# A hybrid pooling and Mamba-2 layer: the last pool gate placed ahead of the output's last part, late products tile by tile, and two sets of weight sums moved into the pool stage

## The chip, the core and the metric

The kernel runs on one core of one Trainium2 chip. The metric is device microseconds of one launch; the figure for a kernel is the median of its runs. The engines are named as the profile names them: PE (matrix products), PEld (its weight loads, which overlap it), DVE (vector), ACT (scalar), POOL (GpSimd, here used nearly only to issue DMAs) and SP (sync, which issues most of the weight loads).

## The reference, cut to what matters

One layer (D = 1024, 512 tokens behind 16 learned ones) with two branches on the same normalised input, merged by gates and followed by an MLP with a squared ReLU:

```python
u = rmsnorm(h, mix_norm_w)
proj = u @ w_in                      # columns: u_pool, z, xBC, dt, gates
gates = sigmoid(proj[..., OFF_GATE:] + b_gate)      # 2 x 1024 columns
# pooling branch: 4 groups of 256 channels, causal mean over 2, 4, 8, 16 tokens
#   minus the input, times a 256 x 256 weight per group, times a scale
y_pool = pool_mixer(u_pool, pool_w_group, pool_scale) @ w_pool_up
# Mamba-2 branch: conv + silu, chunked state-space scan in 8 groups of 256
#   channels, times silu(z), RMS-normalised by group
y_ssd = mamba2_branch(z, xbc, dt_raw, ...) @ w_ssd_out      # 2048 -> 1024
h = h + (gate_pool * y_pool + gate_ssd * y_ssd) @ w_o
v = rmsnorm(h, mlp_norm_w)
hid = relu(v @ w_ff1)                # 1024 -> 4096
h = h + (hid * hid) @ w_ff2          # 4096 -> 1024
out = rmsnorm(h, final_norm_w)
```

## The kernel before, in words

Everything is float32. A product is made of three products of rounded parts: each operand is split into a rounded "hi" half (cast on ACT: yh, whi, ph, ...) and the remainder "lo" (subtraction on DVE: yl, wlo, pl, ...), and hi x hi, lo x hi and hi x lo are added up in PSUM. Some weights go through a seven-product scheme of the Strassen kind; it needs sums of weight blocks. Those of w_ff1 and w_ff2 are made ahead of time by DMAs alone: `weight_steps` (L770) issues, on POOL's queue, copies and accumulating DMAs of 512 KB from one place of device memory to another. A set of w_ff1 ("f1") takes eight of them, in four steps that depend on one another (t1, then t1 += , t2 += t1, t4 += t2), a set of w_ff2 ("f2") four. An accumulating DMA is issued only when the copy under it has landed, and POOL stands in its queue until then. Of the last four sets (f1 4, f2 5, f1 5, f2 6) SETS_POOL (L56) says how many are issued in the pool stage; it is 0 before, and all four follow the load of the residual ht (L1202).

In the order of time:

- **Scan, groups 0 to 7** (to about 474 us): projection, conv, scan and normalisation by group of 256 channels. Each group leaves two tiles of y (y0, y1 of group 0 to y14, y15 of group 7), split into yh and yl at the end of `ssd` (the loop behind `rs`, L719 to L726). A planner of the framework orders the instructions by the order in which they are written, by what they wait for, and by `tc.high_priority` where that is set; `weave` alternates the written order of a scan with that of a filler.
- **The filler of group 7** is `out_part` (L845): w_ssd_out by y8 to y13, in eight output tiles psp0 to psp7 of 128 channels x 512 tokens. They share two PSUM buffers, so psp2 may start when psp0 has been copied out. For each, `add` (L870) copies it on ACT to a tile sp and adds it to `acc_d` in device memory by an accumulating DMA on POOL's queue. psp0 and psp1 are begun before y12 and y13 (group 6) exist; their "late products" (L880 to L883) come when those are there.
- **Pool stage** (474 to 555 us): `pool_pair` makes the u_pool channels of one group of 256 (numbers 3, 2, 1, 0 in that order) by seven products: its weights come as two raw tiles per pair (`raw_block`, L126), are added up on DVE (`sm`, L985 and L987, and back into raw, L989 and L990) and split (whiA, whiS, whiD, whiB on ACT, wlo* on DVE). `averaged` (L962 to L964) makes the causal means on DVE, `pooled_halves` (L973, L974) splits them into ph and pl, `pool_mix` (L1043) multiplies by the group's weight (pg). Between pairs 3 and 2 stand the last part of the output, psl0 to psl7 (y14 and y15 by w_ssd_out, six matmuls each, four PSUM buffers), added to acc0 to acc7 on DVE (L1067), and the last pool gate, `gate_pool(7)`: 24 matmuls into pgp, and a sigmoid on ACT (L759) into m1[7]. The other seven gates have been in device memory since the scan and are loaded to m1 by POOL's queue (L1090).
- **Merge, w_o, MLP** (555 to 1000 us): w_pool_up with the gates, w_o, then ff1 blocks 0 to 3 as plain products, with the start of ff2's seven products woven in (its alpha, L1533, feeds the residual ht on DVE, L1240), then the seven-product MLP.

The weights of w_in-shaped blocks come in a list (`blocks`, filled by `_weight_blocks`) in the order of their use; `block()` takes the next: a raw tile of 128 x 1024 (three buffers, so a load on SP's queue waits until an earlier raw tile's lo half has been made), then whi on ACT (L111) and wlo on DVE (L113).

Of the kernel before, what the change touches and what calls it, by code (L numbers as in the profile page):

```python
# [9 lines left out]
F32 = mybir.dt.float32  # L10
# [4 lines left out]
P = 128  # L15
# [39 lines left out]
PIECES = {4: 21, 7: 14}  # L55
SETS_POOL = 0  # L56

# [7 lines left out]
def kernel(ctx: ExitStack, tc, xT, x, w, fx, f1, f2, vec, fnw, out):  # L65
# [100 lines left out]
    def col(off, i, n=P):  # L166
        return vs[:n, off + i : off + i + 1]
# [426 lines left out]
    def ssd(g, cur):  # L594
# [123 lines left out]
        yield  # L718
        for i in range(2):  # L719
            y = yt[:, i, :]  # L720
            dve.scalar_tensor_tensor(y, y, col(V_SN, 2 * g + i), rs, op0=ALU.mult, op1=ALU.mult)
            yh = yp.tile([P, SEQ], F32R, tag="yh", name=f"yh{g}_{i}")
            yl = yp.tile([P, SEQ], F32R, tag="yl", name=f"yl{g}_{i}")
            act.copy(yh, y)
            dve.tensor_tensor(yl, y, yh.bitcast(F32), op=ALU.subtract)
            ys.append((yh, yl))  # L726
        yield
# [114 lines left out]
    def out_part():  # L842
# [36 lines left out]
        late = [[(next(un), ys[k]) for k in (12, 13)] for d in range(2)]  # L879
        for o in ((0, 0), (1, 0), (0, 1)):  # L880
            for d in range(2):
                for n, (a, b) in enumerate(late[d]):
                    pe.matmul(ps[d], a[o[0]], b[o[1]], start=False, stop=o[1] == 1 and n == 1)  # L883
            yield
        for d in range(2):
            add(ps[d], d)
        for d in range(2, NK):
# [167 lines left out]
    for d in range(NK):  # L1055
        t_load = nc.gpsimd.dma_start(acc[d], acc_d[d])
    for _ in range(SETS_POOL):
        with tc.issue_after(t_load.ins):
            t_load = weight_sums()
    pend = [pooled_halves(*a) for a in pool_pair(POOL_ORDER[0])]  # L1060

    un = units()
    psl_add = []
# [5 lines left out]
    wgb = block(psl_add[2])  # L1069
    gate_pool(NK - 1)  # L1070
    pool_mix(POOL_ORDER[0], pend, wgb)
    nxt = pool_pair(POOL_ORDER[1], psl_add[:2])
    gts = []
    for n in range(1, 4):
# [11 lines left out]
        if n == 1:  # L1086
            for d in MERGE:
                with tc.issue_after(mixed[0].ins):
                    if d < NK - 1:
                        nc.gpsimd.dma_start(m1[d], gate_d[d])  # L1090
    pool_stack.close()
# [602 lines left out]
def _weight_blocks(i):  # L1694
# [9 lines left out]
    def put(b):  # L1704
        blocks.append(b)
# [39 lines left out]
    for t in range(2):  # L1745
        put(cols(w_in, (2 * POOL_ORDER[0] + t) * P))
    blocks += pieces([(d, (14, 15)) for d in range(NK)])
    wg(POOL_ORDER[0] // 2)
    gate(NK - 1)
    for n in range(4):  # L1750
# [95 lines left out]
```

## Time and profile before

| | us |
|---|---|
| three runs | 1001.16, 1000.00, 999.92 |
| median | 1000.0 |
| the profiled execution, its own time | 1001.71 |
| its span on the core | 1000.0 |
| PE busy in the span | 987.8 (99%) |
| DVE busy | 803.9 (80%) |
| ACT busy | 602.2 (60%) |
| POOL busy | 119.5 (12%) |
| granted PE clock | 1.0 in the stages spoken of |

The span is the time from the first to the last instruction in the profiled execution; 1.7 us of that execution's own time lie outside it. A timeline row gives the start, the duration, the engine, the line, the operation with output and inputs, the tile shapes and how many such instructions in a row it stands for; in brackets the idle time ahead of it on its engine, and what ended that. PE is busy 99% of the span, so only some 12 us of it are PE standing still.

### The profile page before, as it was taken

The page shows a single profiled execution, that of the slowest core. Times are in us where ns is not written, and L with a number is a line of the kernel's source. Part 1 is how long each engine was busy: PE and PEld are TensorE (multiplying, and loading weights), DVE is VectorE, ACT ScalarE, POOL GpSimd, SP SyncE. Part 2 cuts the span into 40 slices and gives each one's busy share as a digit, 9 for nine tenths or more (in the row PEclk, how much of TensorE's full clock was granted, in tenths as well). Part 3 has the DMA queues.
Part 4 walks back from the last instruction along what each step waited for, and adds up shares of the span by engine and source line. Part 5 has one row for each costly group of instructions (what it writes and reads, how often), then busy time and mean ns, then how long its engine had stood idle before and what let it go on. Part 6 is the DMA issues. An engine that isn't in the chain of part 4 may idle for free.

```text
span 1000.0 us, 15672 instructions
## 1 busy us (share of the span) xinstructions
PE 987.8 (99%) x6035; PEld 873.8 (87%) x6035; DVE 803.9 (80%) x1162; ACT 602.2 (60%) x855; POOL 119.5 (12%) x215
## 2 busy tenths in 40 slices
PE   9999999999999999999999999999999999999997
PEld 7889998989889999978898888888789999999986
DVE  7978997879845888988789666975988888888885
ACT  7657839495924658574345433477666656656654
POOL 0011321211212212223200001121000000000000
PEclk9999999999999999999999999999999999999999
DMA  7284968666798848768723723899354454454332
GB/s 261 78 254 149 268 197 214 190 191 212 230 271 235 245 129 259 226 163 171 271 85 127 253 85 112 228 243 314 92 190 148 148 190 144 152 186 150 129 106 85
DMA packets 61803, 184.52 MB, mean 185 GB/s; under 512 B 7072, under 2 KB 8416, under 8 KB 60704
## 3 DMA queue, kind: packets, MB, share of 16 engines
q1 hardware_dynamic: 39456, 109.00, 32.7%
q0 software_dynamic: 18240, 67.51, 26.4%
q10 hardware_dynamic: 4032, 7.00, 1.9%
q8 instruction: 47, 0.77, 0.3%
q14 instruction: 28, 0.23, 0.1%
HBM read 173.13 MB, written 58.59 MB: 232 GB/s over the span
## 4 chain that ended last, share of the span: by engine, by line
PE 93%; ACT 3%; DVE 2%; DMA 1%; issue 0%; SPq 0%; ACTq 0%; DVEq 0%
PE px L1465 8%; PE px L215 8%; PE alpha L1533 6%; PE pz L215 6%; PE px L1468 4%; PE px L218 4%; PE alpha L1536 3%; PE pgp L215 3%; PE pz L218 3%; PE pgs L215 3%; PE py L694 2%; PE pqx L509 2%; PE pso L146 1%; PE pgp L218 1%; PE wo_alpha L1226 1%; PE po L688 1%
## 5 line engine op out<-in xcount | busy, mean ns | idle before, releaser
L113 DVE TENSOR_TENSOR wlo<-raw,whi 128x1024 fp32r<-128x1024 f32 (+2 forms) x88 | 102.0, 1171 | 46.8 <-ACT whi L111 31.0
L111 ACT CAST whi<-raw 128x1024 fp32r<-128x1024 f32 (+2 forms) x88 | 87.2, 1011 | 70.3 <-PE pso L147 15.3
L215 PE MATMUL px<-uh,whi 128*128 128x264 f32 (+1 forms) x320 | 80.9, 291 | 0.0
L218 PE MATMUL px<-ul,whi 128*128 128x264 f32 (+1 forms) x320 | 78.8, 285 | 0.0
L1240 DVE TENSOR_TENSOR ht<-ht,alpha 128x1024 f32<-128x1024 f32 x35 | 42.7, 1220 | 29.1 <-PE alpha L1533 29.1
L215 PEld LDWEIGHTS px<-uh,whi 128*128 128x128 f32 x320 | 60.4, 189 | 0.9 <-issue 0.7
L1162 ACT CAST shi<-rawf 128x1024 fp32r<-128x1024 f32 x42 | 44.2, 1053 | 28.0 <-PE alpha L1536 18.3
L218 PEld LDWEIGHTS px<-ul,whi 128*128 128x128 f32 x320 | 60.2, 188 | 0.4 <-issue 0.2
L1533 PE MATMUL alpha<-shi,hh 128*128 128x512 f32 x140 | 55.3, 395 | 2.0 <-DVE ht L1240 1.9
L1536 PE MATMUL alpha<-shi,hl 128*128 128x512 f32 x140 | 54.7, 391 | 0.0
L1163 DVE TENSOR_TENSOR slo<-rawf,shi 128x1024 fp32r<-128x1024 f32 x42 | 51.2, 1219 | 0.6 <-ACT shi L1162 0.6
L1468 PE MATMUL px<-vsl,shi 128*128 128x256 f32 x192 | 47.4, 280 | 0.0
L1465 PE MATMUL px<-vsh,shi 128*128 128x256 f32 x192 | 47.4, 281 | 0.0
L215 PE MATMUL pz<-uh,whi 128*128 128x512 f32 x112 | 43.7, 390 | 0.0
L218 PE MATMUL pz<-ul,whi 128*128 128x512 f32 x112 | 43.6, 389 | 0.0
L215 PE MATMUL px<-uh,wlo 128*128 128x264 f32 (+1 forms) x320 | 41.8, 283 | 0.0
L215 PEld LDWEIGHTS px<-uh,wlo 128*128 128x128 f32 x320 | 39.9, 188 | 0.0
L1533 PE MATMUL alpha<-slo,hh 128*128 128x512 f32 x140 | 37.4, 389 | 0.0
L1465 PEld LDWEIGHTS px<-vsh,shi 128*128 128x128 f32 x192 | 36.2, 188 | 0.9
L1468 PEld LDWEIGHTS px<-vsl,shi 128*128 128x128 f32 x192 | 36.1, 188 | 0.9
L1468 PE MATMUL px<-vl,shi 128*128 128x256 f32 x144 | 36.1, 283 | 0.0
L1465 PE MATMUL px<-vh,shi 128*128 128x256 f32 x144 | 36.0, 282 | 0.0
(599 smaller groups left out, 3064.8 us busy)
## 6 DMA issues: line engine op xcount, KB each, us to landing
raw<-in_w SPq DMA_DIRECT2D x96, 512.0 KB, 4.4
f_t<-in_f POOLq DMA_DIRECT2D x38, 512.0 KB, 7.4
f_s<-in_f POOLq DMA_DIRECT2D x26, 512.0 KB, 7.3
b<-in_f SPq DMA_DIRECT2D x21, 512.0 KB, 4.5
rawf<-in_f SPq DMA_DIRECT2D x36, 256.0 KB, 2.9
rawf<-f_t SPq DMA_DIRECT2D x36, 256.0 KB, 2.9
abc<-acs_d POOLq DMA_DIRECT2D x8, 1024.0 KB, 7.6
f_t<-f_t POOLq DMA_DIRECT2D x12, 512.0 KB, 6.7
```

What stands on the lines that cost most here:

```text
L111: act.copy(hi[:, c], raw[:, c])
L113: dve.tensor_tensor(lo[:, c], raw[:, c], hi[:, c].bitcast(F32), op=ALU.subtract)
L215: pe.matmul(o, wt, rhs[0][k][:, c], start=part == 0 and k == 0, stop=part == 1 and k == NK - 1)
L218: mm[0] = pe.matmul(o, wt, rhs[1][k][:, c], start=False, stop=False)
L509: at = pe.matmul(o, wk, f[k][0], start=start and not low and k == 0, stop=stop and low == 1 and k == 3, skip_group_check=True)
L1162: splits.append((act.copy(hi, src), dve.tensor_tensor(lo, src, hi.bitcast(F32), op=ALU.subtract)))
L1163: dve.tensor_tensor(lo, src, hi.bitcast(F32), op=ALU.subtract)))
L1240: added[0] = dve.tensor_tensor(o, o, src, op=op)
L1465: pe.matmul(ps, m, f[k][0], start=start and not low and k == 0, stop=stop and low == 1 and k == 3, skip_group_check=True)
L1468: pe.matmul(ps, m, f[k][1], start=False, stop=False, skip_group_check=True)
L1533: pe.matmul(ps[t], hh[:, p, seg, st], m, start=bool(first and not low and p == 0), stop=bool(last and low and p == 1), skip_group_check=True)
L1536: pe.matmul(ps[t], hl[:, p, seg, st], m, start=False, stop=False, skip_group_check=True)
```

## The change: what it does

Five edits: SETS_POOL goes from 0 to 2, and the loop that issues those sets moves from behind the loads of acc to behind the last of the seven loads of m1; the loop that makes the last y of group 7 is put under `high_priority`; the late products go tile by tile, all six matmuls of psp0 and then all six of psp1, with `add` of each right behind it under `high_priority`; `gate_pool(7)` is called ahead of the psl loop; and the list of weight blocks is changed to match.

```diff
@@ -53,7 +53,7 @@
 
 SETS_AT = {0: 1, 1: 1, 2: 2, 3: 1, 4: 2, 5: 2, 6: 1, 7: 1}
 PIECES = {4: 21, 7: 14}
-SETS_POOL = 0
+SETS_POOL = 2
 
 PLAIN = 4
 
@@ -716,14 +716,15 @@
         for c in range(4):
             dve.reciprocal(rs[:, ctok(c)], rs[:, ctok(c)])
         yield
-        for i in range(2):
-            y = yt[:, i, :]
-            dve.scalar_tensor_tensor(y, y, col(V_SN, 2 * g + i), rs, op0=ALU.mult, op1=ALU.mult)
-            yh = yp.tile([P, SEQ], F32R, tag="yh", name=f"yh{g}_{i}")
-            yl = yp.tile([P, SEQ], F32R, tag="yl", name=f"yl{g}_{i}")
-            act.copy(yh, y)
-            dve.tensor_tensor(yl, y, yh.bitcast(F32), op=ALU.subtract)
-            ys.append((yh, yl))
+        with tc.high_priority(100) if g == G - 1 else nullcontext():
+            for i in range(2):
+                y = yt[:, i, :]
+                dve.scalar_tensor_tensor(y, y, col(V_SN, 2 * g + i), rs, op0=ALU.mult, op1=ALU.mult)
+                yh = yp.tile([P, SEQ], F32R, tag="yh", name=f"yh{g}_{i}")
+                yl = yp.tile([P, SEQ], F32R, tag="yl", name=f"yl{g}_{i}")
+                act.copy(yh, y)
+                dve.tensor_tensor(yl, y, yh.bitcast(F32), op=ALU.subtract)
+                ys.append((yh, yl))
         yield
 
     late_cast, last_state = [None], {}
@@ -877,13 +878,13 @@
             part(ps[d], d, range(8, 12))
             yield
         late = [[(next(un), ys[k]) for k in (12, 13)] for d in range(2)]
-        for o in ((0, 0), (1, 0), (0, 1)):
-            for d in range(2):
+        for d in range(2):
+            for o in ((0, 0), (1, 0), (0, 1)):
                 for n, (a, b) in enumerate(late[d]):
                     pe.matmul(ps[d], a[o[0]], b[o[1]], start=False, stop=o[1] == 1 and n == 1)
+            with tc.high_priority(100):
+                add(ps[d], d)
             yield
-        for d in range(2):
-            add(ps[d], d)
         for d in range(2, NK):
             ps = psum2(f"psp{d}")[:, :SEQ]
             part(ps, d, range(8, 14))
@@ -1054,11 +1055,9 @@
 
     for d in range(NK):
         t_load = nc.gpsimd.dma_start(acc[d], acc_d[d])
-    for _ in range(SETS_POOL):
-        with tc.issue_after(t_load.ins):
-            t_load = weight_sums()
     pend = [pooled_halves(*a) for a in pool_pair(POOL_ORDER[0])]
 
+    gate_pool(NK - 1)
     un = units()
     psl_add = []
     for d in range(NK):
@@ -1067,7 +1066,6 @@
         psl_add.append(dve.tensor_tensor(acc[d], acc[d], ps, op=ALU.add))
 
     wgb = block(psl_add[2])
-    gate_pool(NK - 1)
     pool_mix(POOL_ORDER[0], pend, wgb)
     nxt = pool_pair(POOL_ORDER[1], psl_add[:2])
     gts = []
@@ -1087,7 +1085,10 @@
             for d in MERGE:
                 with tc.issue_after(mixed[0].ins):
                     if d < NK - 1:
-                        nc.gpsimd.dma_start(m1[d], gate_d[d])
+                        t_load = nc.gpsimd.dma_start(m1[d], gate_d[d])
+            for _ in range(SETS_POOL):
+                with tc.issue_after(t_load.ins):
+                    t_load = weight_sums()
     pool_stack.close()
     tf_stack.close()
     wo_stack = ExitStack()
@@ -1744,9 +1745,9 @@
     blocks += pieces(PARTS)
     for t in range(2):
         put(cols(w_in, (2 * POOL_ORDER[0] + t) * P))
+    gate(NK - 1)
     blocks += pieces([(d, (14, 15)) for d in range(NK)])
     wg(POOL_ORDER[0] // 2)
-    gate(NK - 1)
     for n in range(4):
         if n < 3:
             for i in range(2):
```

No operation is added or taken away. Where the instructions stand on the engines changes in four places. On PE, the late products of the middle part (psp0, psp1 are the output tiles, whi57 and wlo57 the weight, yh6 and yl6 the y of group 6), before:

```order
L883 MATMUL psp0_4664<-yh6_0_4624,whi57_4673 128x512
L883 MATMUL psp0_4664<-yh6_1_4629,whi57_4673 128x512
L883 MATMUL psp1_4665<-yh6_0_4624,whi57_4673 128x512
L883 MATMUL psp1_4665<-yh6_1_4629,whi57_4673 128x512
L883 MATMUL psp0_4664<-yh6_0_4624,wlo57_4674 128x512
L883 MATMUL psp0_4664<-yh6_1_4629,wlo57_4674 128x512
L688 MATMUL po7_0_4756<-ct7_4163,st0_7_4730 128x128
L883 MATMUL psp1_4665<-yh6_0_4624,wlo57_4674 128x512
L883 MATMUL psp1_4665<-yh6_1_4629,wlo57_4674 128x512
L883 MATMUL psp0_4664<-yl6_0_4625,whi57_4673 128x512
L883 MATMUL psp0_4664<-yl6_1_4630,whi57_4673 128x512
L883 MATMUL psp1_4665<-yl6_0_4625,whi57_4673 128x512
```

and now:

```order
L884 MATMUL psp0_4664<-yh6_0_4624,whi57_4673 128x512
L884 MATMUL psp0_4664<-yh6_1_4629,whi57_4673 128x512
L884 MATMUL psp0_4664<-yh6_0_4624,wlo57_4674 128x512
L884 MATMUL psp0_4664<-yh6_1_4629,wlo57_4674 128x512
L884 MATMUL psp0_4664<-yl6_0_4625,whi57_4673 128x512
L884 MATMUL psp0_4664<-yl6_1_4630,whi57_4673 128x512
L688 MATMUL po7_0_4761<-ct7_4163,st0_7_4730 128x128
L884 MATMUL psp1_4665<-yh6_0_4624,whi57_4673 128x512
L884 MATMUL psp1_4665<-yh6_1_4629,whi57_4673 128x512
L884 MATMUL psp1_4665<-yh6_0_4624,wlo57_4674 128x512
L884 MATMUL psp1_4665<-yh6_1_4629,wlo57_4674 128x512
L884 MATMUL psp1_4665<-yl6_0_4625,whi57_4673 128x512
```

psp0 is complete after six of the twelve late products, where it took ten before (psp1's last row is not shown); psp1 is complete after all twelve, as before. The numbers of lines behind L716 are one higher in the new text.

On ACT at the same place (sp0 and sp1 are the copies of those tiles, whi58 to whi60 weights that psp2 and later tiles use, abc7 the decay matrices of group 7's scan), before:

```order
L670 COPY st0_7_4730<-pst7_0_4734 128x256
L647 ACTIVATE abc7_4633<-abc7_4633 128x1024
L849 CAST whi58_4819<-raw58_4818 128x1024
L648 ACTIVATE abc7_4633<-abc7_4633 128x1024
L871 COPY sp0_4811<-psp0_4664 128x512
L871 COPY sp1_4814<-psp1_4665 128x512
L849 CAST whi59_4888<-raw59_4887 128x1024
```

and now:

```order
L670 COPY st0_7_4730<-pst7_0_4734 128x256
L647 ACTIVATE abc7_4633<-abc7_4633 128x1024
L872 COPY sp0_4757<-psp0_4664 128x512
L648 ACTIVATE abc7_4633<-abc7_4633 128x1024
L872 COPY sp1_4785<-psp1_4665 128x512
L850 CAST whi58_4810<-raw58_4809 128x1024
L850 CAST whi59_4878<-raw59_4877 128x1024
```

The copy of psp0 has moved ahead of the cast of whi58 and of the second exponential, and whi58 behind both copies. Further on in ACT's order the two casts yh of group 7 stand behind the copy sp6, where they stood ahead of it; on DVE the last y keeps its place.

On DVE in the pool stage (wlo64 to wlo66 are halves of weights of the gate and of psl, pu6 and pu7 the channels of pair 3, pw their running sums, acc0 the sum with psl0), before:

```order
L113 TENSOR_TENSOR wlo64_5178<-raw64_5176,whi64_5177 128x1024
L113 TENSOR_TENSOR wlo65_5216<-raw65_5214,whi65_5215 128x1024
L1023 TENSOR_TENSOR pu7_5054<-pu7_5054,pxx3_5055 128x264
L1026 TENSOR_TENSOR pu7_5054<-pu7_5054,pz3_5057 128x264
L962 TENSOR_TENSOR pw7_1_5136<-pu7_5054 128x527
L962 TENSOR_TENSOR pw7_2_5138<-pw7_1_5136 128x525
L962 TENSOR_TENSOR pw7_4_5140<-pw7_2_5138 128x521
L962 TENSOR_TENSOR pw7_8_5142<-pw7_4_5140 128x513
L1067 TENSOR_TENSOR acc0_5009<-acc0_5009,psl0_5175 128x512
L964 SCALAR_TENSOR_TENSOR pu7_5054<-pw7_8_5142,pu7_5054 128x512
L962 TENSOR_TENSOR pw6_1_5158<-pu6_5053 128x527
L1067 TENSOR_TENSOR acc1_5010<-acc1_5010,psl1_5189 128x512
```

and now:

```order
L113 TENSOR_TENSOR wlo66_5248<-raw66_5246,whi66_5247 128x1024
L963 TENSOR_TENSOR pw7_1_5136<-pu7_5054 128x527
L963 TENSOR_TENSOR pw7_2_5138<-pw7_1_5136 128x525
L963 TENSOR_TENSOR pw7_4_5140<-pw7_2_5138 128x521
L963 TENSOR_TENSOR pw7_8_5142<-pw7_4_5140 128x513
L965 SCALAR_TENSOR_TENSOR pu7_5054<-pw7_8_5142,pu7_5054 128x512
L963 TENSOR_TENSOR pw6_1_5158<-pu6_5053 128x527
L963 TENSOR_TENSOR pw6_2_5160<-pw6_1_5158 128x525
L963 TENSOR_TENSOR pw6_4_5162<-pw6_2_5160 128x521
L963 TENSOR_TENSOR pw6_8_5164<-pw6_4_5162 128x513
L965 SCALAR_TENSOR_TENSOR pu6_5053<-pw6_8_5164,pu6_5053 128x512
L1066 TENSOR_TENSOR acc0_5009<-acc0_5009,psl0_5207 128x512
```

All ten instructions of the two averages now stand ahead of the first addition to acc; before, the additions lay between them. wlo66 has moved up to before the averages (its row before stood behind the third addition).

On POOL's queue (m1 are the gate loads, ht the residual, f14 and f25 the sets f1 4 and f2 5, f15 the set f1 5), before:

```order
L1090 DMA m1_6_5004<-gate_d6_141 128x512
L1090 DMA m1_3_5001<-gate_d3_138 128x512
L1202 DMA ht_6454<-in_x 128x1024 x4
L777 DMA f14_t1_504<-in_f1 128x1024
L778 DMA f14_s3_505<-in_f1 128x1024
L781 DMA f14_t2_506<-in_f1 128x1024
L779 DMA f14_t1_504<-in_f1 128x1024
L782 DMA f14_s3_505<-in_f1 128x1024
```

and now:

```order
L1088 DMA m1_3_5001<-gate_d3_138 128x512
L778 DMA f14_t1_504<-in_f1 128x1024
L779 DMA f14_s3_505<-in_f1 128x1024
L782 DMA f14_t2_506<-in_f1 128x1024
L780 DMA f14_t1_504<-in_f1 128x1024
L783 DMA f14_s3_505<-in_f1 128x1024
L786 DMA f14_t4_507<-in_f1 128x1024
L785 DMA f14_t2_506<-f14_t1_504 128x1024
```

The twelve DMAs of the sets f1 4 and f2 5 stand behind the m1 loads and ahead of ht; only the sets f1 5 and f2 6 are left behind ht.

On PE, pgp's 24 matmuls stand ahead of the 48 of psl, where they stood behind them.

## The prediction

> **What bounds the kernel now.** I read the page's busy times first, then PE's waits, then the windows by stage.
>
> ```profile
> PE 987.8 (99%) x6035; PEld 873.8 (87%) x6035; DVE 803.9 (80%) x1162; ACT 602.2 (60%) x855; POOL 119.5 (12%) x215
> ```
>
> PE is the bound: 987.8 of a span of 1000.0, so 12.2 us of standing still are all that a reordering can win, and no matmul is taken away. The table of PE's waits says where some of it lies (us in total, times, longest):
>
> ```profile
> PE alpha L1533 <- DVE ht L1240: 1.9, 1, 1.9
> PE psp L146 <- ACT sp L871: 1.5, 1, 1.5
> PE pz L1004 <- ACT pu L1020: 0.3, 1, 0.3
> ```
>
> These three, 3.7 us, are the ones that the change can reach; the rest lies at the start and end of the kernel and in the scan. The windows show how much slack the stages have (window; length, PE, PEld, DVE, ACT, POOL busy; granted clock; DMA share; GB/s):
>
> ```profile
> 500.00:520.00 20.00, 20.00 (x152) 19.35 (x151) 16.67 (x25) 10.60 (x17) 0.00 (x0) 1.00 0.15 55
> 680.00:700.00 20.00, 20.00 (x90) 16.54 (x89) 10.82 (x15) 14.14 (x20) 3.53 (x5) 1.00 1.00 305
> 700.00:724.00 24.00, 23.48 (x104) 19.13 (x102) 23.70 (x38) 14.10 (x21) 0.00 (x0) 1.00 0.34 81
> ```
>
> In the pool stage the DMA engines are nearly empty (0.15) and in the MLP's start full (1.00). The sums are moved from the full place to the empty one. DVE is full behind the full place: 23.70 of 24.00.
>
> My sum is made against the profiled execution's own 1001.71, of which the span is 1000.0; the median of the runs, 1000.0, lies 1.71 below it, and I subtract that at the end. About 0.2%, 2 us, is what a measurement of this kernel can tell from no change.
>
> **Late products tile by tile.** The timeline where psp0 and psp1 end:
>
> ```profile
> 438.79 1.28 PE L883 MATMUL psp<-yh,whi 128*128 128x512 f32 x4
> 439.91 0.61 PE L883 MATMUL psp<-yh,wlo 128*128 128x512 f32 x2
> 440.60 1.06 ACT L647 ACTIVATE abc<-abc 128x1024 f32<-128x1024 f32 x1
> 441.54 1.07 PE L883 MATMUL psp<-yl,whi 128*128 128x512 f32 x4
> 441.55 1.04 ACT L849 CAST whi<-raw 128x1024 fp32r<-128x1024 f32 x1
> 442.49 1.05 ACT L648 ACTIVATE abc<-abc 128x1024 f32<-128x1024 f32 x1
> 443.45 1.05 ACT L871 COPY sp<-psp 128x512 f32<-128x512 f32 x2
> 444.07 0.50 PE L146 MATMUL psp<-yh,whi 128*128 128x512 f32 x1 [1.46 <-ACT sp L871]
> ```
>
> PE ends the twelve late products at 442.6 and stands until sp0 has been copied out, 1.46 us. The copy itself is half of 1.05; it started at 443.45 because ACT did a cast and an exponential first. In the new order psp0 is complete after six of them, where 439.91 + 0.61 gives 440.5, and its copy stands right behind L647, from 441.55 to about 442.15. psp1 still ends at 442.6, so psp2 follows it with no wait: the 1.46 go, **−1.5**. The whi58 cast now stands behind both copies, about 443.6 to 444.6; psp2 reaches whi58 only behind eight matmuls by whi57 and the py and po matmuls of the scan. The added DMA issue on POOL's queue comes earlier with the copies and nobody waits for it. Bounds: 0, if another operand of psp2 or of the scan's products takes the wait's place, to −1.5.
>
> **The last y early.** This part does not do what its words say: DVE's order around the last y is unchanged, and on ACT its two casts now stand behind sp6's copy. They come perhaps 2 us later, and what is queued behind them on ACT (the split of pair 3's weights) with them. The cover is that psl, which needs y14 and y15, now stands behind the gate's 24 matmuls, 5.4 us by the next rows. Cost 0; without that cover up to 2.
>
> **Gate ahead of psl.**
>
> ```profile
> 480.19 1.05 ACT L111 CAST whi<-raw 128x1024 fp32r<-128x1024 f32 x1 [1.39 <-DMA raw<-in_w]
> 481.57 0.39 PE L1004 MATMUL pz<-t1h,whiB 128*128 128x264 f32 x1 [0.26 <-ACT pu L1020]
> 484.55 2.17 DVE L962 TENSOR_TENSOR pw<-pw 128x525 f32<-128x525 f32 x3
> 484.59 0.39 PE L146 MATMUL psl<-yh,whi 128*128 128x512 f32 x1
> 490.27 2.35 DVE L113 TENSOR_TENSOR wlo<-raw,whi 128x1024 fp32r<-128x1024 f32 x2
> 495.49 0.39 PE L215 MATMUL pgp<-uh,whi 128*128 128x512 f32 x1
> 500.93 0.39 PE L146 MATMUL pg<-ph,whi 128*128 128x512 f32 x1
> ```
>
> The wait at 481.57 is for a copy that stood behind a cast that itself waited 1.39 for its load; the copy now stands ahead of that cast: **−0.3** (0 to −0.3). PE then comes to this stage 1.8 us ahead. psl started at 484.59; now 484.59 − 1.8 + (500.93 − 495.49 = 5.4) = 488.2, each tile (495.49 − 484.59)/8 = 1.36. psl5 reuses psl1's buffer, so at 488.2 + 5 × 1.36 = 495.0 it needs acc1's addition. On DVE the averages, ten instructions of about 0.7 (2.17 for three) now stand ahead, behind three wlo of 1.2 (2.35 for two) from about 481: that gives add1's end at about 494.3. Cost 0. A half sum of pair 2's weights also stands ahead of add1; if its raw tile lands late, as in the slowest row of loads below, add1 comes 2.0 later and psl5 waits 1.3. The range of this edit is 0 to +1.3, and the lead of 1.8 is spent below anyway.
>
> **Two sets in the pool stage.** What the sets cost in time on POOL's queue (621.37 is the first issue of f1 4, 639.61 its third step, 656.21 the last issue of f2 5):
>
> ```profile
> 621.37 0.53 POOL L777 DMA_DIRECT2D f_t<-in_f  x1
> 639.61 0.80 POOL L784 DMA_DIRECT2D f_t<-f_t  x1 [3.94 <-DMA f_t<-in_f]
> 656.21 0.82 POOL L782 DMA_DIRECT2D f_s<-in_f  x1 [0.43 <-DMA f_s<-in_f]
> ```
>
> They take 656.21 − 621.37 = 35 us. Behind the m1 loads they start at about 488 and run to about 523, with the third step at 506. In that time two raw loads on SP's queue matter:
>
> ```profile
> 507.19 0.33 SPq L126 DMA_DIRECT2D raw<-in_w  x1
> 511.76 0.69 DVE L985 TENSOR_TENSOR sm<-raw,raw 128x512 f32<-128x512 f32 x1
> 520.39 1.54 SPq L126 DMA_DIRECT2D raw<-in_w  x2
> 524.00 1.06 ACT L132 CAST whiA<-raw 128x1024 fp32r<-128x1024 f32 x1 [3.25 <-DVE pu L1026]
> 528.66 0.68 DVE L974 TENSOR_TENSOR pl<-pu,ph 128x512 fp32r<-128x512 f32 x1
> 530.17 0.39 PE L147 MATMUL pg<-pl,whi 128*128 128x512 f32 x1
> ```
>
> The load issued at 507.19 feeds the sum at 511.76. From there DVE works nearly without a gap to the end of pl at 529.34 (17.6 us), which PE takes at 530.17: 0.83 of margin. With L for the time from issue to landing, and the issue some 0.2 earlier, pl ends at 507.0 + L + 17.6, and PE is L − 5.6 late against before, but no better than its lead of −1.8. What L is, by the DMA rows (KB, median us to landing), in windows 500 to 520, 480 to 500, 450 to 480, 250 to 300 and 660 to 700:
>
> ```profile
> raw<-in_w SPq DMA_DIRECT2D x2, 512.0 KB, 3.6
> raw<-in_w SPq DMA_DIRECT2D x3, 512.0 KB, 4.4
> raw<-in_w SPq DMA_DIRECT2D x4, 512.0 KB, 6.7
> raw<-in_w SPq DMA_DIRECT2D x7, 512.0 KB, 7.5
> raw<-in_w SPq DMA_DIRECT2D x5, 512.0 KB, 9.7
> ```
>
> 3.6 is a load alone, 9.7 one beside dense sums and MLP loads. At 507 the set f1 4 is in its dependent end, one or two transfers in flight, so I take the row that is nearest, 4.4 beside the m1 loads, and put some on it: L = 5.0. Then PE's lead at 530 is −0.6 instead of −1.8: this edit **costs 1.2** here (0 at L = 3.6; +2.9 at 6.7; +5.9 at 9.7).
>
> The page "DMA: Bandwidth & Descriptors" of the Trainium skill, section "Queues, rings and completion order", states that each DMA engine goes round between the queue rows that have work, packet by packet. It speaks against this change: a raw load beside the sums would get half the engines' time. In the trace 9.7 against 3.6 bears that out in direction; at half rate for the data alone, with 512 KB at some 400 GB/s, an estimate from it is L = 4.9, and the sum would be 0.1 better.
>
> **What their leaving brings at 723.** The stall of 1.9 at alpha L1533 is PE waiting for DVE, which is full from 700 on. DVE's backlog begins with a hole:
>
> ```profile
> 673.15 1.43 SPq L95 DMA_DIRECT2D raw<-in_w  x2
> 686.24 1.05 ACT L111 CAST whi<-raw 128x1024 fp32r<-128x1024 f32 x1 [4.04 <-DMA raw<-in_w]
> 687.33 1.23 DVE L113 TENSOR_TENSOR wlo<-raw,whi 128x1024 fp32r<-128x1024 f32 x1 [5.40 <-ACT whi L111]
> ```
>
> A weight issued at 673.15 landed 13 us later beside the last two sets, and DVE stood for 5.40. With two sets gone, the other two run from about 621 to 656 and the load meets them no more: at 7.5 it lands at 680.7, 5.5 earlier, and DVE starts its backlog about 4 earlier, more than the stall: **−1.9** (0 to −1.9).
>
> **The sum.** −1.5 − 0.3 + 1.2 − 1.9 = −2.5: 1001.71 − 2.5 = 999.2 in the profiled execution's terms, 997.5 as a median. With L from 3.6 to 6.0 the forecast's own range is 996.3 (−3.7) to 998.5 (−1.5).
>
> **Rivals.**
> - *One load late* (0.20): the load of 507 takes 6.7, as in the window from 450 to 480, where sums and additions to acc_d ran beside it. PE is 1.1 late at 530, the stall at 723 goes: 1.1 − 1.9 = −0.8, 999.2. For it: the sums are the same kind of traffic. Against it: their steps depend on one another, and the DMA share in this stage was 0.15.
> - *The stall at 723 stays* (0.12): DVE's backlog from 700 is bound by its own work and not by the hole at 682, or the freed engines bring other loads forward which take the same time. Then −0.6, 999.4. For it: DVE is busy 23.70 of 24.00 there, so the hole must carry through 36 us to matter.
> - *Slower: both loads late* (0.20). The loads of 507 and of 520 both feed the chain to pl, the second through whiA at 524.00, 3.6 behind its issue. If the sums still flow at 520, both delays add up: the second lands L − 4.8 later for the first and L − 3.6 for itself, less the margin of 0.83, 2L − 9.2 in all. At 7.5 that is +5.8, less 1.9 at 723: +3.9, 1003.9. It ends slower than before from L = 5.6 and over 0.2% slower from 6.6. For it: twelve DMAs in 35 us reach 523. Against it: alone in the stage they should be through sooner than the 35 us which they took beside other loads.
>
> **Chances and range.** My forecast has 0.48, the rivals 0.20, 0.12 and 0.20. The forecast lies more than 2 us below the median but for its upper end, so faster is 0.45; that end and the two rivals inside 2 us make 0.35; slower is 0.20. The range goes from 996.0, just below all gains with no cost, to 1002.0, at which the third rival begins to be over 0.2%: that leaves out most of that rival and little else. The forecast and the first two rivals alone lie within 996.0 to 999.5.
>
> **What would show it.** Right: no wait of PE at psp2 (before 1.46), the copy sp0 at about 441.6; no wait at pz; psl at about 488, without a wait ahead of psl5; pg's pl at 530 or just before, and the load feeding the third pair's sum landing in about 5 us; the sets' POOL rows from 488 to about 523; no raw load of 13 us at 673 and no wait at alpha L1533. Wrong: a wait of PE for pl or for pu between 510 and 545, which would mean L above 5.6; a hole of DVE ahead of sm; or the stall at alpha unchanged or moved to another ht.

## The result, and the profile after

The changed kernel takes 1006.63 us (median of 4 runs, 1005.60 to 1009.38) against 1000.58 (999.92 to 1001.93) of the kernel before, measured beside it: a ratio of 1.0064, with a 95% interval of 1.0052 to 1.0077. It is slower by 0.64%, and the time lies above the range of the prediction. The profiled execution of the changed kernel took 1009.38 with a span of 1007.7, the longest of its four; against the span before it has 7.7 us more, and the account below is of these; the medians lie 6.0 apart.

The busy times on the page of the changed kernel:

```profile
span 1007.7 us, 15675 instructions
PE 991.4 (98%) x6035; PEld 875.4 (87%) x6035; DVE 804.3 (80%) x1162; ACT 601.6 (60%) x855; POOL 119.9 (12%) x215
```

PE has the same 6035 matmuls and is busy 3.6 us longer (991.4 against 987.8), and it stands still for 16.3 instead of 12.2, 4.1 more. So there are two things to find: new waits, and matmuls that became slower. PE's waits in the changed kernel (us in total, times, longest):

```profile
PE psl L146 <- ACT m L760: 3.0, 1, 3.0
PE pg L147 <- DVE pl L975: 1.8, 2, 1.2
...
PE pg L146 <- ACT ph L974: 1.2, 1, 1.2
...
PE pxx L1005 <- ACT pu L1012: 0.9, 1, 0.9
PE psl L146 <- DVE acc L1066: 0.8, 1, 0.8
```

The three waits that the change aimed at, psp 1.5, pz 0.3 and alpha 1.9, are gone. In their place stand 3.8 at psl, 0.9 at a pxx (at 509.78, behind a cast on ACT that waited 1.39 for DVE) and 3.0 at pg. 3.8 + 0.9 + 3.0 − 3.7 = +4.0, which is the idle time. The windows of the same kernel (window; length, PE, PEld, DVE, ACT, POOL busy; granted clock; DMA share; GB/s):

```profile
474.00:500.00 26.00, 22.20 (x130) 19.21 (x129) 18.07 (x26) 10.64 (x15) 10.59 (x18) 1.00 0.90 314
500.00:520.00 20.00, 19.13 (x135) 17.88 (x134) 17.52 (x26) 7.49 (x12) 2.69 (x4) 1.00 0.90 245
520.00:540.00 20.00, 17.01 (x94) 14.19 (x94) 15.15 (x25) 6.75 (x11) 1.67 (x2) 0.90 0.54 143
540.00:560.00 20.00, 20.00 (x123) 18.30 (x122) 17.24 (x25) 11.21 (x18) 0.00 (x0) 0.93 0.40 132
700.00:724.00 24.00, 24.00 (x108) 19.88 (x107) 21.87 (x35) 14.94 (x20) 0.00 (x0) 1.00 0.20 67
```

and two of them in the kernel before:

```profile
520.00:540.00 20.00, 20.00 (x136) 18.57 (x135) 19.89 (x30) 10.74 (x18) 0.00 (x0) 1.00 0.29 98
540.00:560.00 20.00, 20.00 (x100) 16.97 (x99) 15.66 (x22) 9.64 (x13) 0.00 (x0) 1.00 0.61 203
```

The DMA share of the pool stage from 500 to 520 went from 0.15 to 0.90: the sums fill the empty place. PE's granted clock, 1.00 there before, is 0.90 and 0.93 from 520 to 560: 0.10 × 20 + 0.07 × 20 = 3.4 us of slower matmuls, nearly all of the 3.6. At 700 PE now works through.

**At psl.** The timeline of the changed kernel, the rows of ACT, DVE and PE:

```profile
484.16 1.05 ACT L111 CAST whi<-raw 128x1024 fp32r<-128x1024 f32 x1 [5.54 <-DMA raw<-in_w]
485.25 1.23 DVE L113 TENSOR_TENSOR wlo<-raw,whi 128x1024 fp32r<-128x1024 f32 x1 [5.04 <-ACT whi L111]
488.53 0.70 DVE L963 TENSOR_TENSOR pw<-pu 128x527 f32<-128x527 f32 x1
495.62 0.68 DVE L1066 TENSOR_TENSOR acc<-acc,psl 128x512 f32<-128x512 f32 x1
487.87 0.39 PE L146 MATMUL psl<-yh,whi 128*128 128x512 f32 x1
496.45 0.47 PE L146 MATMUL psl<-yh,whi 128*128 128x512 f32 x1 [2.98 <-ACT m L760]
498.90 0.49 PE L146 MATMUL psl<-yh,whi 128*128 128x512 f32 x1 [0.82 <-DVE acc L1066]
```

PE comes to psl at 487.87 (488.2 was forecast) and to psl4 at 493.47. ACT and DVE stood for over 5 us, since a raw tile landed only at 484.16. DVE, which works in order, begins the averages at 488.53 and reaches the addition of psl0 at 495.62 to 496.30. The row at 496.45 names the sigmoid of m as releaser, which also ended just then (496.42). In the list of instructions psl4's first matmul waits for the addition to acc0 and its weight, not for that sigmoid; e9 below tests which it is.

**At pg.** The timeline of the changed kernel, POOL's and SP's queues, ACT, DVE and PE:

```profile
521.93 0.84 POOL L780 DMA_DIRECT2D f_t<-in_f  x1 [8.88 <-DMA f_t<-in_f]
523.23 0.82 POOL L783 DMA_DIRECT2D f_s<-in_f  x1 [0.45 <-DMA f_s<-in_f]
523.75 1.54 SPq L126 DMA_DIRECT2D raw<-in_w  x2
532.33 1.05 ACT L132 CAST whiA<-raw 128x1024 fp32r<-128x1024 f32 x1 [8.25 <-DMA raw<-in_w]
533.41 1.23 DVE L133 TENSOR_TENSOR wloA<-raw,whiA 128x1024 fp32r<-128x1024 f32 x1 [4.85 <-ACT whiA L132]
534.22 0.50 PE L146 MATMUL pg<-ph,whi 128*128 128x512 f32 x1 [1.24 <-ACT ph L974]
535.89 0.80 PE L147 MATMUL pg<-pl,whi 128*128 128x512 f32 x1 [1.16 <-DVE pl L975]
```

The load that was issued at 520.39 and cast at 524.00 is now issued at 523.75 and cast at 532.33: 8.6 from issue to cast where it was 3.6. The last two accumulating DMAs of the second set went out just ahead of it, at 521.93 and 523.23. ACT stands 8.25 for it, DVE 4.85, and PE comes to pg with both its operands late. Then the clock, in windows of one us (columns as above):

```profile
534.00:535.00 1.00, 0.50 (x1) 0.19 (x1) 1.00 (x2) 1.00 (x3) 0.00 (x0) 1.00 0.02 8
535.00:536.00 1.00, 0.11 (x1) 0.11 (x1) 1.00 (x3) 0.28 (x1) 0.00 (x0) 0.94 0.00 0
536.00:537.00 1.00, 1.00 (x2) 0.39 (x2) 1.00 (x3) 0.00 (x0) 0.00 (x0) 0.50 0.00 0
...
541.00:542.00 1.00, 1.00 (x5) 0.81 (x4) 1.00 (x2) 0.19 (x2) 0.00 (x0) 0.50 0.00 0
542.00:543.00 1.00, 1.00 (x7) 1.00 (x7) 0.78 (x2) 0.63 (x1) 0.00 (x0) 0.65 0.00 0
```

Behind those waits the clock is 0.50 from about 535.9 to 542.7, 6.8 us at half speed: this is the 3.4.

The account of the profiled execution: −3.7 (psp, pz, alpha) + 3.8 (psl) + 0.9 (pxx) + 3.0 (pg) + 3.4 (clock) = +7.4 of 7.7.

### The profile page after: what moved, and what is told of

Read it like the earlier page. It is cut to its first block, busy times and chain, and to the rows that moved or that the text cites. A ratio compares the mean times of both kernels' runs of the same rounds, so it can differ in the third digit from the quotient of the medians.

```text
span 1007.7 us, 15675 instructions
## 1 busy us (share of the span) xinstructions
PE 991.4 (98%) x6035; PEld 875.4 (87%) x6035; DVE 804.3 (80%) x1162; ACT 601.6 (60%) x855; POOL 119.9 (12%) x215
## 4 chain that ended last, share of the span: by engine, by line
PE 89%; DVE 4%; ACT 3%; DMA 3%; issue 1%; SPq 0%; ACTq 0%; DVEq 0%
PE px L1466 8%; PE px L215 8%; PE alpha L1534 6%; PE pz L215 6%; PE px L1469 4%; PE px L218 4%; PE alpha L1537 3%; PE pz L218 3%; PE pgp L215 3%; PE pgs L215 3%; DMA raw<-in_w 2%; PE pqx L509 2%; PE py L694 2%; PE po L688 2%; PE pso L146 1%; PE wo_alpha L1227 1%
```

## The experiments

My theory after these readings: the second set of sums in the pool stage costs most, by the one load at 520 and the clock behind it; the late products cost a little, because the raw tile at 484 lands late and DVE hands back psl's buffers late; the gate's place costs nothing by itself. The rivals: the gate's place or the m1 loads cause the wait at psl; psl4 waits for the sigmoid; either set would do the harm. The ratios are to the kernel before, run on the same chip, with 95% intervals. In every kernel below the `high_priority` around the last y is left out unless the text of the edit shows it: in the changed kernel the order of the instructions on all five engines is the same with it and without it, so this fifth edit does nothing.

### Each edit alone

**e1_late**: the late products' new order only.

```diff
-        for o in ((0, 0), (1, 0), (0, 1)):
-            for d in range(2):
+        for d in range(2):
+            for o in ((0, 0), (1, 0), (0, 1)):
...
+            with tc.high_priority(100):
+                add(ps[d], d)
```

> Late products tile by tile alone, the rest as before. Two theories of the wait ahead of psl4 in the changed kernel (3.0 us, and 0.8 ahead of psl5). Theory 1: it comes from the gate's new place, which puts the averages ahead of the additions to acc on DVE; then this kernel shows no wait at psl and only the gains at 444 and 481: -1.8, about 998.2. Theory 2: it comes from the late products, whose new order puts the last y's casts behind sp6, frees raw tiles 2 us later and lets the gate loads run beside the load of psl's first weight, which so lands at 484 and not at 480; then psl0, which stands in front here, waits until about 485.2 where PE would come at 482.8: 2.4 lost, about 1000.6.

Measured 1.0012 (1.0001 to 1.0022). The tile that lands late (later expectations call it 65) is psl's second weight here, for psl4 to psl7, and its first only in the kernels with the gate ahead; the expectation above took it for the first. The waits and the timeline of e1:

```profile
PE psl L146 <- DVE acc L1067: 3.6, 2, 2.0
483.99 1.05 ACT L111 CAST whi<-raw 128x1024 fp32r<-128x1024 f32 x1 [5.40 <-DMA raw<-in_w]
485.07 1.23 DVE L113 TENSOR_TENSOR wlo<-raw,whi 128x1024 fp32r<-128x1024 f32 x1 [4.90 <-ACT whi L111]
```

The tile is late and DVE has its hole with no gate moved and no sums: the second theory held in its cause, though it is psl4 (1.98) and psl7 (1.64) that wait and not psl0. The late products alone lose at psl (3.6) what they win at psp, pz and alpha (3.7).

**e2_gate**: only the gate ahead of psl, with its weight block.

```diff
+    gate_pool(NK - 1)
...
-    gate_pool(NK - 1)
```

> The gate ahead of psl alone. Theory 1 (the order on DVE suffices): a wait of about 3 ahead of psl4, +3 to +3.8, about 1003.5. Theory 2 (the order costs only when the load of psl's first weight lands late): that load lands at 480 as before, the averages end about 492 and add0 by 493, psl4 comes at 495.4 and does not wait: 999.7 to 1000.2.

Measured 1.0000 (0.9988 to 1.0011). No wait at psl; the addition to acc0 and the first matmul of psl4 in e2's timeline:

```profile
492.81 0.68 DVE L1068 TENSOR_TENSOR acc<-acc,psl 128x512 f32<-128x512 f32 x1
496.35 0.39 PE L146 MATMUL psl<-yh,whi 128*128 128x512 f32 x1
```

The addition starts 2.8 earlier than in the changed kernel, and PE comes to psl 3.0 later (490.91 against 487.87), so it ends 2.9 ahead of psl4. The second theory held: the gate's place by itself costs nothing. This run does not show what it costs when PE comes early. By an estimate from these rows, with PE at psl4 at 493.47 and at psl5 1.36 later, as in the changed kernel, the addition to acc0 (ended at 493.49 here) would be just in time and that to acc1 (495.89) about 1 late. The wait at alpha is gone here too, though the sets are where they were.

**e3_sums**: only the two sets, in the pool stage.

```diff
-SETS_POOL = 0
+SETS_POOL = 2
...
+            for _ in range(SETS_POOL):
+                with tc.issue_after(t_load.ins):
+                    t_load = weight_sums()
```

> Two sets of sums in the pool stage alone. Theory 1 (the sums delay the raw load of 520 by about 5 us wherever the stage stands): waits of PE at pg of about 3 and a lower granted clock behind them, 3 more; the stall at alpha goes, -1.9: about 1004. Theory 2 (the load was late only because the stage came 3.5 us later and met the accumulating steps of the second set): the load lands in about 5, no wait at pg over 1, the stall at alpha goes: about 998.5.

Measured 1.0038 (1.0025 to 1.0050): the largest single part. The waits, the timeline and a window of e3:

```profile
PE pg L147 <- DVE pl L974: 2.3, 2, 1.2
PE pg L146 <- ACT ph L973: 0.9, 1, 0.9
520.93 1.54 SPq L126 DMA_DIRECT2D raw<-in_w  x2
529.03 1.05 ACT L132 CAST whiA<-raw 128x1024 fp32r<-128x1024 f32 x1 [8.25 <-DMA raw<-in_w]
520.00:540.00 20.00, 16.78 (x87) 13.74 (x86) 15.62 (x24) 6.27 (x11) 0.76 (x1) 0.91 0.50 132
```

The load goes out at nearly the old time (520.93 against 520.39) and takes 8.1: the harm at pg and the half clock behind it (0.91) come from the sets, not from the time at which PE or SP come there. The first theory held.

### Parts together

**e4_late_sums**: e1 and e3 together.

```diff
-SETS_POOL = 0
+SETS_POOL = 2
```

> Late products and sums, without the gate's move. If the parts add up: the first run's figure plus the third's difference. By theory 1 of both: -1.8 + 4 = 1002.2; by theory 2 of both: +0.6 - 1.5 = 999.1.

Measured 1.0047 (1.0034 to 1.0060), about the sum of the two parts (1.0012 and 1.0038) and dearer than either theory had it: psl waits 3.3, pg 2.8, and the clock is 0.91 from 520 to 540. The two losses lie some 40 us apart and add up.

**e10_late_gate**: the changed kernel without the sets in the pool stage.

```diff
-SETS_POOL = 2
+SETS_POOL = 0
```

> The change without the two sets in the pool stage: late products and the gate's place. Theory 1 (the wait at psl has nothing to do with the sums): 3.0 ahead of psl4 and 0.8 ahead of psl5 as in the changed kernel, no wait at pg, clock 1.00 through 560; the 1.8 of 444 and 481 and the stall at alpha set against 3.8: 1001 to 1002. Theory 2 (the sums slowed psl's loads too): waits at psl under 2, 999 to 1000.

Measured 1.0015 (1.0006 to 1.0024), within the first theory's range. There is no wait at pg, as it said, but one wait at psl instead of two, and the clock, which it had at 1.00, falls behind it, here in e10's timeline and windows:

```profile
495.89 0.47 PE L146 MATMUL psl<-yh,whi 128*128 128x512 f32 x1 [2.38 <-DVE acc L1068]
497.00:498.00 1.00, 1.00 (x3) 0.45 (x2) 1.00 (x2) 0.00 (x0) 0.00 (x0) 0.50 0.00 0
498.00:499.00 1.00, 1.00 (x3) 0.70 (x3) 1.00 (x3) 0.00 (x0) 0.00 (x0) 0.50 0.00 0
```

The sigmoid ended at 495.48 here and the addition to acc0 at 495.75, and the same wait is now put down to the addition.

**e11_one_set_all**: the changed kernel with one set in the pool stage.

```diff
-SETS_POOL = 2
+SETS_POOL = 1
```

> The whole change, but one set instead of two in the pool stage. If the second set's accumulating steps at 520 are what the pool stage lost: no wait at pg over 0.5, clock 1.00, and the time of the run without sets, 1001 to 1002. If the stage is 3 to 4 us later here and one set is enough to meet the loads: waits at pg of 1 and more, 1003 to 1005.

Measured 1.0020 (1.0011 to 1.0029). No wait at pg; at psl 2.06 and 1.10, with the clock at 0.50 from about 497 to 504. So of the 0.64% of the change, the second set alone is 0.44. The whole change is also 0.17% above e4, which leaves out only the gate's move; the intervals overlap, e1, e2 and e10 show no cost of that move, and what makes the difference, if there is one, is not shown.

### What holds psl back

**e9_adds_first**: the changed kernel with the first two additions ahead of the second average on DVE.

```diff
+        with after(averages.get(2 * POOL_ORDER[0])):
+            psl_add.append(dve.tensor_tensor(acc[d], acc[d], ps, op=ALU.add))
+        if d == 1:
+            with after(psl_add[d]):
+                first_pair[0] = averaged(*first_pair[0])
+            pend = [pooled_halves(*a) for a in first_pair]
```

> The changed kernel with one difference: on DVE the additions of psl0 and psl1 to acc stand ahead of pair 3's second average (five operations), and the other additions behind it. Theory 1 (psl4 and psl5 wait for the PSUM buffers of psl0 and psl1, which these additions release): no wait ahead of psl4 and psl5; the waits turn up at psl6 and psl7, whose additions now come later. Theory 2 (the profile's own word: psl4 waits for the sigmoid of the gate on ACT): the wait of 3.0 ahead of psl4 stays. Either way the time is near the changed kernel's, 1005 to 1008, since nothing is taken from DVE.

psl4 goes without a wait, at 493.67, 2.8 earlier than in the changed kernel and 3.0 before the sigmoid ends here (496.69): the buffer's release by the addition was the cause, and the sigmoid named in the profile was only the last event before. But the wait moved on to psl5 and psl6. The first matmuls of psl4, psl5 and psl6 in e9's timeline:

```profile
493.67 0.39 PE L146 MATMUL psl<-yh,whi 128*128 128x512 f32 x1
497.45 0.50 PE L146 MATMUL psl<-yh,whi 128*128 128x512 f32 x1 [2.26 <-DVE acc L1066]
502.07 0.80 PE L146 MATMUL psl<-yh,whi 128*128 128x512 f32 x1 [2.10 <-DVE acc L1066]
```

The addition to acc1, for which psl5 waits, stands behind a sum that waits 2.85 for its load, and the one for psl6 behind the second average, so the first theory had psl5 wrong. Further waits follow at pxx (3.2 and 1.9), and the clock is 0.87 from 500 to 520 and 0.83 from 520 to 540: 1.0120 (1.0107 to 1.0133), much worse than either theory said. This other order of the same work on a full engine did not help.

**e5_late_ycast**: e1, with the casts of the last y held ahead of the copies sp6 and sp7 on ACT, as before the change.

```diff
+            y_cast[g] = act.copy(yh, y)
...
+            with after(y_cast.get(G - 1) if d >= 6 else None):
+                act.copy(o, ps)
```

> The late products tile by tile as in the first run, with one thing put back: the two casts yh of group 7 stand ahead of the copy sp6 on ACT again. The first run lost 3.6 us at psl because the raw tile 65 (there psl's second weight) landed at 484.0 instead of 480.2, and DVE stood for it with the averages and the additions to acc behind. Theory 1 (the casts behind sp6 free the raw tiles 2 us late, and that is the greater part): tile 65 is issued at about 474 and lands by 481.5, the waits ahead of psl fall under 1 us, the gain of 1.8 stays: about 2 below before. Theory 2 (the gate loads to m1, which run beside it 5 us earlier than before, are the greater part): it lands at about 482.5, waits of about 2 stay: as before.

The tile is issued at 474.75 instead of 475.91 and cast at 481.70 instead of 483.99, but not all of that is the order: this whole execution runs 0.5 earlier there (the last y starts on DVE at 465.65, in e1 at 466.14). Counted from that start, the load goes out 9.1 later here, 9.8 in e1 and 8.2 in the kernel before, so putting the casts back undoes 0.7 of 1.6. And psl still waits 2.7, in three pieces, and the ratio is 1.0019 (1.0011 to 1.0028), no better than e1, where the first theory had 2 us below before. The landing is a part of the cause and not the whole.

**e6_late_mheld**: e1, with the m1 loads held back until the weight of the fifth psl tile is split.

```diff
+        pairs = [(next(un), ys[k]) for k in (14, 15)]
+        if d == 4:
+            held = pool.tensor_copy(seen, pairs[0][0][1].bitcast(F32)[:, :1])
...
-                with tc.issue_after(mixed[0].ins):
+                with tc.issue_after(held.ins):
```

> The late products as in the first run, with the seven gate loads to m1 held until the lo half of weight 65 is made (by a one-column copy on POOL that reads it). Theory 1 (the late issue of the raw tile is the greater part): tile 65 still lands near 483, waits of 2.5 to 3.6 stay, 1 above before. Theory 2 (the gate loads beside it): it lands at about 481.5, waits under 1.5, 1 to 2 below before.

The cast is still at 484.07, psl still waits 2.5 (1.97 and 0.48), and the ratio is 1.0026 (1.0017 to 1.0036); the clock, 1.00 there in e1, is 0.58 from 490 to 494. The load takes 8.1 from issue to cast with the m1 loads held back and without (e1), so they are not why the tile is late; that rival falls.

**e13_lo_behind**: e5, with the low halves of the two weight tiles behind the psl weights (the gate's and pair 2's) split only after the fourth addition.

```diff
-        proj(narrow(ps), block(), X if first else U)
+        proj(narrow(ps), block(behind), X if first else U)
...
-    wgb = block(psl_add[2])
-    gate_pool(NK - 1)
+    wgb = block(psl_add[3])
+    gate_pool(NK - 1, behind=psl_add[3])
```

> As the fifth run (late products, casts yh put back), with the lo halves of the two weights behind psl (66 and 67, 2.35 us on DVE) moved from ahead of the fourth addition to acc to behind it. Theory 1 (the order on DVE decides: psl7 waited 1.67 for an addition that stood behind work nobody needed yet): that wait goes, the two of 0.5 stay, 0.5 to 1.5 below before. Theory 2 (DVE's whole work from tile 65's landing to the end of the stage bounds it in any order): the wait turns up behind psl, at pgp or pg, and the time is the fifth run's, 1 above before.

Measured 1.0004 (0.9992 to 1.0016), the lowest of the kernels with the late products and the sets unmoved, though its interval overlaps theirs. In its timeline one wait at psl is left:

```profile
489.39 0.47 PE L146 MATMUL psl<-yh,whi 128*128 128x512 f32 x1 [1.20 <-ACT pu L1031]
```

The later wait (1.67 in e5) is gone, so it came from the two splits ahead of the additions. The first one stays: the tile was cast at 483.06 in this run, and the addition to acc0 ended at 489.25, just ahead of the matmul. Neither theory holds whole: the wait did not turn up behind psl, as the second had it, but the time is not below before, as the first had it. The wait at psl has both causes, the late tile and the order on DVE.

### Where the sets can stand

**e7_one_set**: e3 with one set instead of two.

```diff
-SETS_POOL = 0
+SETS_POOL = 1
```

> The sums alone, with one set (f1 4) instead of two in the pool stage; it is through by about 515. Theory 1 (the accumulating steps of the second set at 520 make the raw load of 520 late, and the waits that follow halve PE's granted clock): no wait at pg over 0.5, clock 1.00 in 520 to 560, no loss: 0 to 2 below before. Theory 2 (the traffic at 507 already costs, by the load of 507 and DVE's chain): a wait of 1 to 2 at pg remains, 1 to 2 above before.

Measured 0.9991 (0.9980 to 1.0002). No wait at pg, the clock 1.00, no wait at alpha, as the first theory had it. e7's timeline:

```profile
525.37 1.05 ACT L132 CAST whiA<-raw 128x1024 fp32r<-128x1024 f32 x1 [3.21 <-DMA raw<-in_w]
```

The load of the disputed place goes out at 521.80 and is cast 3.6 later, as in the kernel before: the one set issued its last DMA at 512.09, nearly ten microseconds ahead of it.

**e8_sets_later**: both sets, but started only behind pair 1's mix, by a small copy on POOL that reads its output.

```diff
+        if n == 2:
+            at = pool.tensor_copy(seen, yps[2 * POOL_ORDER[n]][0].bitcast(F32)[:, :1])
+            with after(t_load, at):
+                for _ in range(SETS_POOL):
+                    weight_sums()
```

> Two sets alone, but held until pair 1 has been mixed (a one-column copy on POOL that reads yph2), so from about 540. If the loss lies only in the meeting with the raw load of 520: no wait at pg, clock 1.00, and the MLP's first loads as free as in the third run, so no stall at alpha: 1 to 2 below before. If the sums cost wherever raw loads run: a new wait between 545 and 600, 2 or more above before.

Measured 0.9990 (0.9982 to 0.9999), a gain of a tenth of a per cent, and the only interval that ends below 1, by little and as one of fourteen. The sets start at 546.29; the load is cast at 523.84 on time, and nothing waits at pg or at alpha.

**e12_best**: the whole change, with the casts of e5 and the sets of e8.

> All parts with the two faults mended: the casts yh ahead of sp6, and the two sets held until pair 1 has been mixed. The raw tile 65 lands near 481.7 as in the fifth run, the averages end about 493.5, so psl4 waits 0.5 to 1.5 instead of 3.0; no wait at pg; no stall at alpha. By the sum -1.8 + 1.5 - 1.0 (the eighth run's difference): 1 to 1.5 below before. If DVE's work between 481 and 500 bounds the stage whatever the order is, the whole 1.8 goes there: 1 below before, as the eighth run.

Measured 1.0010 (1.0001 to 1.0019). No wait at pg. But the tile is cast at 483.44, not near 481.7 as expected, psl waits 2.76 and 0.69, and the clock is 0.50 from about 498 to 505. With the gate ahead, PE comes to psl with DVE as late as ever; the expectation fell.

**e14_both**: e13 and the sets of e8.

> The same with the two sets held until pair 1 has been mixed, as in the eighth run. By theory 1: 1 to 2.5 below before. By theory 2: as before.

Measured 0.9991 (0.9982 to 1.0000): psl waits 1.47, nothing at pg or alpha. This is e8's time; what the late products win at psp is spent again at psl, and e8 alone is as good with less.

## Why the prediction was wrong, step by step

- **Late products, −1.5 and −0.3: right at the place.** psp0 is copied from 441.71 (forecast 441.55), psp2 starts at 442.60 without a wait, and none is left at pz. The prediction had the −0.3 under the gate's move; e1, without that move, has no wait at pz, and e2, with it alone, has 1.0. e1 shows what it brought in the end: nothing, 1.0012.
- **The last y, "The cover is that psl, which needs y14 and y15, now stands behind the gate's 24 matmuls … Cost 0": the first step that failed.** It saw that the split of pair 3's weights comes late with the casts, and asked only who needs y. What came late was the raw tile whose load is issued behind the delayed work: 475.94 instead of 473.98, and its cast at 484.16 against 480.19 for the tile of that load before. It is the edit of the late products that delays the casts, since e1, without the edit around the last y, has the same. Counted from the start of the last y on DVE, this load goes out 8.2 later in the kernels with the old order (before, e2, e3, e7, e8), 9.8 later with the late products, and 9.1 later where the casts are put back (e5, e12, e13, e14). It then takes 6.2 to 7.0 to its cast with the old order and 7.0 to 8.2 with the late products. e6 shows that the m1 loads are not the reason.
- **Gate ahead, "that gives add1's end at about 494.3. Cost 0", with 1.3 at most: failed.** PE came when forecast (487.87); the step let DVE run from about 481, and it stood 5.04 until 485.25, so that the averages began at 488.53 and the first addition, which psl4 needed at 493.47, ended at 496.30. The waits were 3.0 and 0.8. e2, where the first addition ended at 493.49, has none, but there PE came 3.0 later; that the working would have held with the tile on time is an estimate, with about 1 us of wait at psl5, and not shown. That pair 2's raw tile might come late was named; that it would be the tile in front was not.
- **Two sets, L = 5.0 for the load of 507: the wrong load.** The sum sm behind that load ran with no wait. The load of 520 took 8.6. The step took the traffic for thin ("one or two transfers in flight"), where the DMA share from 500 to 520 was 0.90, and did not price the load of 520, which met the second set's accumulating DMAs of 521.93 and 523.23. The third rival had the right kind of mechanism, two loads beside the sums, and the side of the result, at 0.20; its price of 5.8 comes near the 3.0 of waits and 3.4 of clock only by luck, since one load was late and not two, and it had no clock in it. e7 and e8 show that it is the second set at this place that costs.
- **The clock: a term that the sum did not have.** A row of granted clock of 1.00 was read as a property of the stage. Waits that follow each other took it to 0.50 for 6.8 us, 3.4 of the 6.4 that pg cost.
- **The stall at alpha, −1.9: right in sign, and the cause only in part.** The hole of DVE ahead of 693 shrank from 5.40 to 1.24. But the stall is gone in e1 and e2 as well, which leave the sets where they were: there the raw loads of 660 to 700 still take 9.0 and 8.5 by the DMA rows, and the hole shrank all the same (1.77 and 1.25). So its going cannot be credited to the sets alone. It seems to have hung on how one load met one set, so that a shift of a microsecond or two undid it; that is argued and not shown. e13 has 0.6 of it. The second rival, that the stall stays, fell.

What stays open: why the tile's load takes longer behind the late products. Its three raw loads go out within 2.4 us there and within 5.2 in the kernel before, and the loads of acc run beside them; no run holds either back. The medians of e5 and e1 do not tell whether an earlier landing is worth anything.

## What to carry to other kernels

When an edit brings the busiest engine to a stage earlier, ask what must come earlier with it: the instruction that hands back its PSUM buffer, on an engine that works in order, and the raw tile that this engine waits for in front of it. For an instruction that moves later, ask what load its buffer frees, not only who reads its result. A stage with empty DMA engines (0.15) can still hold a load with about a microsecond of margin (0.83 by the rows before; in e3 a load that was 4.5 late made 3.2 of waits); put background transfers by those loads, and price a run of short waits with the clock that may fall behind it.

## What the runs showed of the hardware

PE's granted clock fell to half behind short waits though PE never stood for long in one piece: in e3 PE was busy 0.15, 0.42, 0.40, 0.33 and 0.59 in the five microseconds from 530, no single wait was over 1.2, and the clock was 0.50 from about 535 to 538.5. In e10 one wait of 2.38 was enough, and in the changed kernel one of 2.98 (493.47 to 496.45) was not: its windows from 493 to 498 all show 1.00. So it is not the longest wait that decides.

What decides shows when PE's busy time is read in the stretches in which the clock changes. Half rate lasts 3.41 us in e3, e4, e6 and e10 and 6.83 in the changed kernel, e9, e11 and e12, so the clock appears to be set anew every 3.41 us, at moments that lie otherwise in each execution. Here are such stretches (columns as above), three with the clock's fall at their end (e10, e12, the changed kernel) and two without (the changed kernel, e5):

```profile
493.10:496.52 3.42, 1.04 (x5) 0.57 (x4) 3.35 (x6) 3.37 (x5) 0.00 (x0) 1.00 0.01 2
494.35:497.76 3.41, 1.51 (x6) 1.05 (x6) 3.38 (x6) 2.65 (x4) 0.00 (x0) 1.00 0.00 0
532.46:535.88 3.42, 1.03 (x4) 0.29 (x2) 2.47 (x4) 2.82 (x5) 0.00 (x0) 1.00 0.29 120
...
494.92:498.33 3.41, 1.63 (x6) 1.05 (x6) 3.33 (x7) 2.51 (x4) 1.38 (x3) 1.00 0.25 100
493.16:496.57 3.41, 1.74 (x8) 1.43 (x8) 3.41 (x7) 0.00 (x0) 0.00 (x0) 1.00 0.81 249
```

PE was busy for 0.30, 0.44 and 0.30 of the first three and for 0.48 and 0.51 of the last two. In all sixteen traces, from 25 us on, the clock fell behind every stretch at full rate in which PE was busy 0.44 or less, nine of them ahead of the last 25 us, and behind none with 0.48 or more. The wait of 2.98 was spread over two stretches (busy 0.58 and 0.48) and did no harm; the wait of 2.38 lay in one.

The Trainium skill, "TensorE: Matmul & The Clock Gate", section "Part 1: The HAM clock gate (the "warmup" mystery)", states half rate after at least one idle window of about 3.4 us, in a window that runs freely. The half rate agrees with the 0.50 here, and the window with the 3.41 and its place, which differs from execution to execution; that the window must be idle does not agree, since PE was busy for 0.16 to 0.44 of the nine.

A load of 512 KB took 3.6 from issue to cast in the kernel before and in e7, and 8.1 to 8.6 beside the end of the two sets (e3, the changed kernel), at the same place in the program: the end of a set, which the prediction took for thin traffic, more than doubled it.
